# Hybrid decoder trunk on one core: token-major weight units of 4 k-tiles x 512 columns in place of 8 x 256, and new prices for TensorE in the scheduler

## Chip, core and metric

The kernel runs on one core of one Trainium2 chip. The metric is the device time of one execution in microseconds (us); lower is better. The kernel before takes 1906.26 us (median of three runs).

## The reference

Two layers over 256 tokens of width 1024, all in float32. Cut to its frame:

```python
for l in range(2):
    h = h + 0.5 * rmsnorm(swiglu(rmsnorm(h, g[0]), ffn1_gate[l], ffn1_up[l], ffn1_down[l]), g[1])   # width 2816
    u = rmsnorm(h, g[2])
    q, k, v, z, xBC, dt_raw, gate_pre = split(u @ w_in[l])       # 1536, 1536, 1536, 2048, 4096, 32, 2048 columns
    y_att = dilated_attention(q, k, v)                           # 3 dilation groups x 8 heads of 64
    y_ssd = ssd_branch(z, xBC, dt_raw, ...)                      # conv of 4 taps, silu, Mamba-2 SSD in 8 groups, gate by silu(z), norm
    gates = sigmoid(gate_pre + b_gate[l])
    h = h + rmsnorm((gates[0] * (y_att @ w_att_out[l]) + gates[1] * (y_ssd @ w_ssd_out[l])) @ w_o[l], g[3])
    h = h + rmsnorm(memory_cross_attention(rmsnorm(h, g[4]), rmsnorm(mem, mem_norm_g[l]), ...), g[5])   # 4 heads of 256
    h = h + 0.5 * rmsnorm(swiglu(rmsnorm(h, g[6]), ffn2_gate[l], ffn2_up[l], ffn2_down[l]), g[7])
```

## The kernel before

**Weights.** All weight matrices are cut into units of 1 MB ([128 partitions] x [2048 float32]). `PLAN` lists the units in the order in which they are used. A unit is brought in as two halves (`raw`, 512 KB each, three buffers), and each half is split into a high part `wh` (ScalarE, a copy to float32r) and a low part `wl` (VectorE, `raw - wh`). Five units fit at once (`NBUF`). Each product is three float32r matmuls (`mm3`): high x high, high x low, low x high.

**Two forms of product.** *Feature-major* (`feat_major`): the weight tile is the stationary operand, 256 tokens of `x` stream past it; q, k, bc, xs, most of the FFN's gate and up, xa_wq and xa_wk. *Token-major* (`tok_major`): a tile of `x` (128 tokens of one k-tile of 128 features) is stationary and the weight's columns stream past it; dt and v, the gates, z, xa_wv and the first two units (`FF_TOK`) of each FFN's gate and up. In the kernel before a token-major unit holds all 8 k-tiles of 256 columns, so a matmul streams 256 columns, and a unit is worked off for token block `t = 0` and then `t = 1`. The row units (`row_mm`: down, att_out, ssd_out, w_o, xa_wo) stream 512 columns of the weight past a tile of the hidden values, into tiles `acc`.

**Order.** One Python program writes the instructions of all engines. TensorE (PE) follows the main line; everything else (norms, evacuations, attention heads, SSD groups) runs in generator tasks that are advanced by `tick()`. Each engine has a clock of its own in the program, moved on by prices (`pe_cost`, `act_cost`, `dve_cost`, ...); a task's instruction is written down when its inputs are ready by these clocks (for PE: `MARGIN` = 300 ns earlier). So the prices decide behind which main-line matmul a task's transpose or matmul stands. On the chip each engine works its own list in order.

**Places that the prediction speaks of.** (a) *Norm chains*: after the last `acc` matmul of a row unit group, `boundary` computes, for each token block, squares (ACT), product with the gain (DVE, `pg`), root (POOL), new `h` (DVE), squares again, root, `xn` (DVE), and then PE transposes `xn` into `xT`. While the chain of `t = 1` runs, PE works on things that do not need it: the `t = 0` pass of the next FFN's first units (tile `gu`), of dtv and v, or, behind w_o, the values of the memory (tile `xv`, unit xa_wv). (b) *SSD groups* (`ssd`, `group_units`): for each of 8 groups the matmuls `BC` and `xs` are followed by a convolution and silu (tile `conv`, ACT and DVE), whose results PE takes up in `cb` and `xsT`; later `y` goes through a norm and is transposed (`yT`). (c) The *start*, where the first weights are still on their way.

```python
MARGIN = 300
def wait(*aps, tag="ps", n=1):
    while not has(tag, n) or PE.at(aps) + MARGIN > now():
        yield
```

Of the kernel before, what the change touches and what calls it, by code (L numbers as in the profile page):

```python
# [38 lines left out]
def ffn_plan(name, l):  # L39
    p = []  # L40
    for j in range(FF_UNITS):
        p += [(name + "_gate", l, j), (name + "_up", l, j)]
        if j == FF_TOK:
            p += [(name + "_down", l, i) for i in range(FF_TOK - 1)]
        if FF_TOK <= j <= FF_UNITS - SPLIT:
            p.append((name + "_down", l, j - 1))
    return p + [(name + "_down", l, FF_UNITS - SPLIT + i) for i in range(SPLIT)]


def plan():  # L50
    p = []
    for l in range(DEPTH):
        p += ffn_plan("ffn1", l)
        p += [("dtv", l, 0), ("dtv", l, 1)] + [("v", l, i) for i in (1, 3)]
        p += [("q", l, 2 * g) for g in range(3)] + [("k", l, 2 * g) for g in range(3)]
        p += [("v", l, i) for i in (0, 2, 4)]
# [13 lines left out]
        p += [("ssd_out", l, 7), ("xa_wk", l, 3), ("xa_wv", l, 0)] + [("w_o", l, u) for u in range(4)]  # L70
        p += [("xa_wv", l, 1), ("xa_wv", l, 2)] + [("xa_wq", l, u) for u in range(4)] + [("xa_wv", l, 3)]
# [3 lines left out]


PLAN = plan()


@with_exitstack  # L80
def tile_trunk(ctx: ExitStack, tc: tile.TileContext, x, mem, gains, hparams, chparams, b_gate, wts, out):
# [265 lines left out]
    def get(name, l, i):  # L347
# [8 lines left out]
        k, n = dict(dtv=(4, 1152)).get(name, (2 if name in ROWS else KB, 2048))  # L356
# [42 lines left out]
    def xk(xx, k, cols):  # L399
        tiles = xx[k // 2]  # L400
        return tiles[0][:, k % 2, cols], tiles[1][:, k % 2, cols]

# [127 lines left out]
    def ffn(name, l, xx, ready, make_chain, early=lambda: None):  # L530
# [10 lines left out]
        def act_tok(j, t, p):  # L541
            s = t2("hm0", (128, 256))
            yield from ACT("activation", s, p[:, 0], AF.Silu)
            yield from DVE("tensor_mul", s, s, p[:, 1])
            give(p)
            yield from wait(s)
            pt = ps("hT", (128, 2, 128))
            for i in range(2):
                yield from PE("transpose", pt[:, i], s[:, blk(i)], ident)
            yield from split(hts[j][0][:, :, tok(t)], hts[j][1][:, :, tok(t)], pt)  # L550
# [6 lines left out]
        w0 = [None] * FF_TOK  # L557
        for t in range(2):
            for j in range(FF_TOK):
                if t == 0:  # L560
                    w0[j] = [get(name + "_gate", l, j), None]
                    new_h(j)
                p = un("gu")
                tok_major(p[:, 0], w0[j][0], xx, t)
                if t == 0:
                    w0[j][1] = get(name + "_up", l, j)
                tok_major(p[:, 1], w0[j][1], xx, t)
                if t == 1:
                    drop(w0[j][0])
                    drop(w0[j][1])  # L570
                pend[j] = spawn(act_tok(j, t, p))
        acc = None

        def down(j):
            until(pend[j])
# [58 lines left out]
    def mix(l, xx, ready, params, kv):  # L634
# [66 lines left out]

        wd = {}
        for t in range(2):
# [8 lines left out]
            for j in (2, 4):  # L712
                if t == 0:
                    wd[j] = get("v", l, j - 1)
                p = un("v1", (128, 512))
                tok_major(p[:, :256], wd[j], xx, t)
                if t == 1:
                    drop(wd[j])
                spawn(evac_v(j, t, p, 0))
        decay_task = spawn(decays(dt_raw))  # L720

        def late_v():
            for i in (0, 2, 4):
                w = get("v", l, i)
                p = un("v")
                for t in range(2):
                    tok_major(p[:, t], w, xx, t)
                drop(w)
                spawn(evac_v(i + 1, None, p, 0))
# [105 lines left out]
        def gate_act(p, bg, u, res):  # L835
            g = t2("gate")
            yield from DVE("tensor_tensor", g, p, bg[:, None, u * 256:u * 256 + 256].to_broadcast([128, 2, 256]), op=ALU.add)
            give(p)
            yield from ACT("activation", g, g, AF.Tanh, scale=0.5)
            res[u] = g  # L840

        def gate_unit(which, bg, u, res):
            w = get(f"gate{which}", l, u)
            p = un("gate")
            for t in range(2):
                tok_major(p[:, t], w, xx, t)
            drop(w)
            spawn(gate_act(p, bg, u, res))

        m0, g1 = [None] * 4, [None] * 4  # L850
        bg = gate_bias(0)
        for u in range(4):
            gate_unit(0, bg, u, m0)
        bg = gate_bias(1)
        gate_unit(1, bg, 0, g1)
# [17 lines left out]
        def z_gate(p, res):  # L873
            zt = t2("zt")
            yield from ACT("activation", zt, p, AF.Silu)
# [3 lines left out]
        def decay_block(g, W, cbm, rz):  # L879
# [11 lines left out]
            while not rz:  # L891
# [8 lines left out]
        def ssd(g, rBC, rxs, rz, yy):  # L900
# [4 lines left out]
            decay = spawn(decay_block(g, W, cbs, rz))  # L905
# [50 lines left out]
            while not rz:  # L956
                yield
            yield from DVE("tensor_tensor", y[:, 1], y[:, 1], yo, op=ALU.add)
            yield from DVE("tensor_tensor", y, y, rz[0], op=ALU.mult)
# [23 lines left out]
        def group_units(g):  # L983
            rBC, rxs, rz, yy = [], [], [], []
# [11 lines left out]
            w = get("z", l, g)  # L996
            p = un("z")
            for t in range(2):
                tok_major(p[:, t], w, xx, t)
# [288 lines left out]
```

## Time and profile before

| | |
|---|---|
| runs | 1905.03, 1906.26, 1909.02 us (median 1906.26) |
| profiled execution, first to last instruction (its span) | 1903.0 us; its own whole time is not given beside it, the runs' median is 3.3 us above the span |
| TensorE matmul busy | 1880.4 us, 99% of the span, 13620 matmul records |
| TensorE weight load busy | 93% |
| VectorE / ScalarE / GpSimd busy | 63% / 52% / 11% |
| granted TensorE clock, mean | 0.999 of full |
| HBM traffic | 330.9 MB, mean 174 GB/s over the span |

Matmuls are pipelined and their recorded durations overlap (a 256-column matmul has a duration of 283 ns and the next one starts 120 ns later), so what a matmul costs is read from the distance between starts, not from its duration or the busy share.

### The profile page before, as it was taken

What the parts mean: (1) busy time and instruction counts of PE and PEld (TensorE: products, weight loads), DVE (VectorE), ACT (ScalarE), POOL (GpSimd) and SP (SyncE); (2) the same over time, 40 slices, a digit from 0 to 9 for tenths busy, and PEclk for the clock granted to TensorE, in tenths of its full rate; (3) what the DMA queues carried; (4) which work ended last, traced back from release to release, by engine and by line L of the source; (5) the groups of instructions that cost most, each with busy time, mean ns of one, the idle gap of its engine ahead of it and who ended that gap; (6) DMA issues with size and microseconds to landing.
All of it is one profiled execution on the core that took longest, in us unless ns stands there. A gap on an engine that the chain in (4) does not pass through costs nothing.

```text
span 1903.0 us, 33128 instructions
## 1 busy us (share of the span) xinstructions
PE 1880.4 (99%) x13620; PEld 1763.9 (93%) x13620; DVE 1192.1 (63%) x1729; ACT 995.9 (52%) x1488; POOL 212.2 (11%) x244
## 2 busy tenths in 40 slices
PE   7999999999999999999999999999999999999998
PEld 6999899899999989999999999898999999999997
DVE  5555654568787865655465546535878777765553
ACT  5444654456666654544354436444566664654542
POOL 0000000032342000000000000000332420000000
PEclk9999999999999999999999999999999999999999
DMA  6655453355565554565556546443555556545652
GB/s 212 217 192 194 158 186 116 118 174 181 182 198 170 172 199 145 175 218 184 178 177 218 182 160 210 134 156 121 166 190 176 168 189 207 171 139 176 223 192 77
DMA packets 107720, 333.09 MB, mean 175 GB/s; under 512 B 10864, under 2 KB 27568, under 8 KB 107568
## 3 DMA queue, kind: packets, MB, share of 16 engines
q1 hardware_dynamic: 107568, 330.97, 53.3%
q8 instruction: 107, 1.75, 0.4%
q14 instruction: 45, 0.37, 0.1%
HBM read 329.81 MB, written 1.11 MB: 174 GB/s over the span
## 4 chain that ended last, share of the span: by engine, by line
PE 92%; DVE 2%; DMA 2%; ACT 2%; POOL 1%; issue 1%; SPq 0%; DVEq 0%; POOLq 0%; ACTq 0%
PE acc L210 22%; PE u L210 11%; PE g L210 11%; PE gate L210 5%; PE xs L210 5%; PE gu L210 4%; PE z L210 4%; PE BC L210 4%; PE q L210 4%; PE k L210 4%; PE v L210 2%; PE xq L210 2%; PE o L210 2%; DMA raw<-in_wts 2%; PE xv L210 2%; PE xk L210 2%
## 5 line engine op out<-in xcount | busy, mean ns | idle before, releaser
L210 DVE TENSOR_TENSOR wl<-raw,wh 128x1024 fp32r<-128x1024 f32 (+1 forms) x588 | 704.9, 1216 | 332.1 <-ACT wh L210 330.1
L210 ACT ACTIVATE wh<-raw 128x1024 fp32r<-128x1024 f32 (+1 forms) x588 | 610.2, 1050 | 443.6 <-DMA raw<-in_wts 231.9
L210 POOL TENSOR_SCALAR ab<-ab,nacs 128x128 f32<-128x128 f32 x128 | 134.4, 1066 | 465.4 <-DMA ab<-acsD 465.4
L210 PE MATMUL g<-xTh,wh 128*128 128x256 f32 x576 | 163.2, 283 | 0.0
L210 PE MATMUL u<-xTh,wh 128*128 128x256 f32 x576 | 163.0, 283 | 0.0
L210 PE MATMUL u<-xTl,wh 128*128 128x256 f32 x576 | 163.0, 283 | 0.0
L210 PE MATMUL u<-xTh,wl 128*128 128x256 f32 x576 | 163.0, 283 | 0.0
L210 PE MATMUL g<-xTh,wl 128*128 128x256 f32 x576 | 163.0, 283 | 0.0
L210 PE MATMUL g<-xTl,wh 128*128 128x256 f32 x576 | 163.0, 283 | 0.0
L210 PE MATMUL acc<-wl,hth 128*128 128x512 f32 x352 | 137.5, 390 | 0.0
L210 PE MATMUL acc<-wh,htl 128*128 128x512 f32 x352 | 137.4, 390 | 0.0
L210 PE MATMUL acc<-wh,hth 128*128 128x512 f32 x352 | 137.3, 390 | 0.0
L210 PEld LDWEIGHTS g<-xTl,wh 128*128 128x128 f32 x576 | 110.5, 192 | 0.9
L210 PEld LDWEIGHTS g<-xTh,wh 128*128 128x128 f32 x576 | 110.5, 192 | 0.9
L210 PEld LDWEIGHTS u<-xTh,wh 128*128 128x128 f32 x576 | 110.6, 192 | 0.0
L210 PEld LDWEIGHTS u<-xTl,wh 128*128 128x128 f32 x576 | 110.6, 192 | 0.0
L210 PEld LDWEIGHTS u<-xTh,wl 128*128 128x128 f32 x576 | 110.6, 192 | 0.0
L210 PEld LDWEIGHTS g<-xTh,wl 128*128 128x128 f32 x576 | 110.5, 192 | 0.0
L210 DVE SCALAR_TENSOR_TENSOR conv<-raw_xbc,chp,conv 128x255 f32<-128x255 f32 (+2 forms) x192 | 81.9, 488 | 0.0
L210 PEld LDWEIGHTS acc<-wh,htl 128*128 128x128 f32 x352 | 66.1, 188 | 13.7
L210 PEld LDWEIGHTS acc<-wh,hth 128*128 128x128 f32 x352 | 66.2, 188 | 12.9
L210 PEld LDWEIGHTS acc<-wl,hth 128*128 128x128 f32 x352 | 66.2, 188 | 12.7
(260 smaller groups left out, 5169.5 us busy)
## 6 DMA issues: line engine op xcount, KB each, us to landing
raw<-in_wts SPq DMA_DIRECT2D x580, 512.0 KB, 4.5
gain<-in_gains SPq DMA_DIRECT2D x18, 512.0 KB, 6.4
ab<-acsD SPq DMA_DIRECT2D x32, 256.0 KB, 6.0
raw<-in_wts SPq DMA_DIRECT2D x8, 288.0 KB, 3.4
gain<-in_b_gate SPq DMA_DIRECT2D x4, 512.0 KB, 6.8
mem<-in_mem SPq DMA_DIRECT2D x8, 256.0 KB, 4.9
out_h<-h SPq DMA_DIRECT2D x4, 256.0 KB, 2.7
h<-in_x SPq DMA_DIRECT2D x2, 256.0 KB, 2.9
```

Source lines behind the costliest of these rows:

```text
L210: return getattr(self.eng, what)(*a, **k)
```

## The change

1. **Layout.** A token-major unit (`WIDE`: z, both gates, xa_wv, the values but for 512 of the 1536 columns, and the first two gate and up units of each FFN) holds 4 k-tiles of 512 columns. Two units make one block of 512 columns: a pass over token block `t` takes the first unit's four k-tiles and then the second's, into one PSUM tile of 128 x 512. Both units stay until `t = 1` is through. Bytes, number of units, splits and DMAs are as before.
2. **What follows from it.** z comes in blocks of two groups (after `xs` of the even groups), gate1 in two blocks (before the groups, and after group 3), the memory's values in two blocks of two heads (the first with the keys, the second behind w_o; before, two units stood behind w_o and one behind the queries). The silu of the FFN's first units and the merges work on 128 x 512. `y * silu(z)` becomes two multiplies of 256 in place of one of 512.
3. **Prices.** `pe_cost`: a float32r matmul of n columns is priced at n/2.4 + 13.4 ns, before n/2.4 + 2.5; transposes and float32 matmuls change by little.

```diff
@@ def plan()
-        p += [("gate0", l, u) for u in range(4)] + [("gate1", l, 0)]
+        p += [("gate0", l, u) for u in range(4)] + [("gate1", l, u) for u in range(2)]
...
-            p.append(("z", l, g))
-            if g in (2, 4, 6):
-                p.append(("gate1", l, g // 2))
+            if g % 2 == 0:
+                p += [("z", l, g), ("z", l, g + 1)]
+            if g == 3:
+                p += [("gate1", l, 2), ("gate1", l, 3)]
...
+WIDE = ("vw", "gate0", "gate1", "z", "xa_wv")
+
+def wide(name, i):
+    return name in WIDE or name.endswith(("_gate", "_up")) and i < FF_TOK
@@ def pe_cost(op, out, ins, k)
+        m, n = size(ins[0]), size(ins[1])
         if op == "transpose":
-            cycles = 256
-        elif ins[0].dtype == F32R:
-            cycles = size(ins[1])
-        else:
-            m = size(ins[0])
-            cycles = 4 * max(m, size(ins[1])) * (m / 128 if m == 64 else 1)
-        return cycles / 2.4 + 2.5
+            return 109
+        if ins[0].dtype == F32R:
+            return n / 2.4 + 13.4
+        return 2 * max(112, 2 * n / 2.4 + (28 if m == 64 else 3))
@@
+    def wide_units(name, l, b, xx, done):
+        ws = [get(name, l, 2 * b)]
+        for t in range(2):
+            p = un(name, (128, 512))
+            tok_major(p, ws[0], xx, t, 0, 4)
+            if t == 0:
+                ws.append(get(name, l, 2 * b + 1))
+            else:
+                drop(ws[0])
+            tok_major(p, ws[1], xx, t, 4, 4)
+            if t == 1:
+                drop(ws[1])
+            done(t, p)
@@ def ffn(...)
         for t in range(2):
-            for j in range(FF_TOK):
...
-                tok_major(p[:, 0], w0[j][0], xx, t)
...
-                tok_major(p[:, 1], w0[j][1], xx, t)
...
+            for m in ("_gate", "_up"):
+                p = un("gu", (128, 512))
+                for i in range(2):
+                    if t == 0:
+                        w0[m].append(get(name + m, l, i))
+                    tok_major(p, w0[m][i], xx, t, 4 * i, 4)
+                    if t == 1:
+                        drop(w0[m][i])
@@ def group_units(g)
-            w = get("z", l, g)
-            p = un("z")
-            for t in range(2):
-                tok_major(p[:, t], w, xx, t)
-            drop(w)
-            spawn(z_gate(p, rz))
+            if g % 2 == 0:
+                wide_units("z", l, g // 2, xx, lambda t, p: spawn(z_gate(p, rz)))
@@
         value(1)
-        value(2)
-        O, heads = xattn(l, xq, K, V, value)
+        O, heads = xattn(l, xq, K, V)
```

**Where the instructions stand, first place: TensorE behind w_o of layer 0**, where the values of the memory (`xv` before, `xa_wv` in the change) run while the chain of `t = 1` computes `xn`; `xT` are the transposes that take `xn` up. Before, 72 rows of `xv` stand between the last `acc` row of w_o and the first of these rows' `xT`:

```order
L210 MATMUL xv<-wh,memh 128x256
L210 MATMUL xv<-wl,memh 128x256
L210 MATMUL xv<-wh,meml 128x256
L210 MATMUL xT<-ident,xn 128x128 x4
L210 MATMUL xv<-wh,memh 128x256
L210 MATMUL xv<-wl,memh 128x256
```

In the change 33 rows of `xa_wv` stand there, of twice the columns:

```order
L215 MATMUL xa_wv<-wh,memh 128x512
L215 MATMUL xa_wv<-wl,memh 128x512
L215 MATMUL xa_wv<-wh,meml 128x512
L215 MATMUL xT<-ident,xn 128x128 x4
L215 MATMUL xa_wv<-wh,memh 128x512
L215 MATMUL xa_wv<-wl,memh 128x512
```

The first `xT` of `t = 1` moved from behind 72 x 256 columns to behind 33 x 512. In the same way it stands behind 33 `gu` rows in place of 72 at the first units of ffn2 (both layers) and of ffn1 in layer 1; behind dtv it stands after 24 rows `dtv` and 24 of `v` (512 columns) in place of 24 `dtv` and 42 of `v` (256). The chains of `t = 0`, which run behind the last 48 `acc` rows, are taken up after 26 `acc` rows in place of 28 at w_o (both layers).

**Second place: VectorE in the same stretch**, the chain of `t = 1` itself (`h_93` is the half of `h` that belongs to `t = 1`; `wl` rows are weight halves between its steps). Before:

```order
L210 TENSOR_TENSOR pg<-acc,gain 128x512
L210 TENSOR_TENSOR wl<-raw,wh 128x1024
L210 TENSOR_TENSOR pg<-acc,gain 128x512
L210 SCALAR_TENSOR_TENSOR h_93<-pg,r,h_93 128x512
L210 TENSOR_TENSOR wl<-raw,wh 128x1024
L210 SCALAR_TENSOR_TENSOR h_93<-pg,r,h_93 128x512
L210 TENSOR_TENSOR wl<-raw,wh 128x1024
L210 SCALAR_TENSOR_TENSOR xn<-h_93,r,gain 128x512 x2
```

In the change:

```order
L215 TENSOR_TENSOR pg<-acc,gain 128x512
L215 TENSOR_TENSOR wl<-raw,wh 128x1024
L215 TENSOR_TENSOR pg<-acc,gain 128x512
L215 SCALAR_TENSOR_TENSOR h_93<-pg,r,h_93 128x512
L215 TENSOR_TENSOR wl<-raw,wh 128x1024
L215 SCALAR_TENSOR_TENSOR h_93<-pg,r,h_93 128x512
L215 TENSOR_TENSOR wl<-raw,wh 128x1024
L215 SCALAR_TENSOR_TENSOR xn<-h_93,r,gain 128x512 x2
```

Nothing moved on VectorE: the same three weight halves stand between the same steps. The same holds at the first units of ffn2 in both layers, of ffn1 in layer 1, and behind w_o in layer 1.

**Third place: TensorE in SSD group 2 of layer 0**, between the end of ssd_out (`acc<-..,yh`) and `cb`, which takes up the convolution of `BC`. Before (nine more `xs` rows follow, and then `cb`):

```order
L210 MATMUL acc<-wh,yh 128x512
L210 MATMUL acc<-wl,yh 128x512
L210 MATMUL acc<-wh,yl 128x512
L210 MATMUL xs<-xTh,wh 128x256
L210 MATMUL xs<-xTl,wh 128x256
L210 MATMUL xs<-xTh,wl 128x256
L210 MATMUL yT<-ident,y 128x128 x4
L210 MATMUL xs<-xTh,wh 128x256
L210 MATMUL xs<-xTl,wh 128x256
L210 MATMUL xs<-xTh,wl 128x256
```

In the change:

```order
L215 MATMUL acc<-wh,yl 128x512
L215 MATMUL xs<-xTh,wh 128x256
L215 MATMUL xs<-xTl,wh 128x256
L215 MATMUL xs<-xTh,wl 128x256
L215 MATMUL xs<-xTh,wh 128x256
L215 MATMUL xs<-xTl,wh 128x256
L215 MATMUL xs<-xTh,wl 128x256
L215 MATMUL cb<-conv 128x128 x2
```

`cb` moved from behind 15 `xs` rows (and the transposes `yT`, which now stand among the `BC` rows ahead) to behind 6. In group 0, `xsT` stands after 22 rows of `z` (512 columns) and `cb` in place of 48 rows of `z` (256), `cb` and 3 of the next `BC`.

## Rows read from the trace of the kernel before

**Rows 1.** The page of the profile: TensorE's line of the busy times, and the chain that ended last as shares of the span by engine.

```profile
PE 1880.4 (99%) x13620; PEld 1763.9 (93%) x13620; DVE 1192.1 (63%) x1729; ACT 995.9 (52%) x1488; POOL 212.2 (11%) x244
PE 92%; DVE 2%; DMA 2%; ACT 2%; POOL 1%; issue 1%; SPq 0%; DVEq 0%; POOLq 0%; ACTq 0%
```

**Rows 2.** The timeline of TensorE in the middle of ffn2, layer 0: start in us from the span's start, duration, engine, line, operation, output and inputs, shape. 24 matmuls of 512 columns start from the first row to just before the second, 48 of 256 columns from the third to just before the fourth.

```profile
827.48 0.40 PE L210 MATMUL acc<-wh,hth 128*128 128x512 f32 x1
...
832.95 0.28 PE L210 MATMUL g<-xTh,wh 128*128 128x256 f32 x1
...
838.70 0.28 PE L210 MATMUL u<-xTh,wh 128*128 128x256 f32 x1
...
844.46 0.40 PE L210 MATMUL acc<-wh,hth 128*128 128x512 f32 x1
```

**Rows 3.** Groups of TensorE's instructions by name and shape: the high x high third of each token-major group (xcount; busy us, mean ns of one; idle before).

```profile
L210 PE MATMUL gate<-wh,xTh 128*128 128x256 f32 x256 | 76.1, 297 | 0.0
L210 PE MATMUL gu<-wh,xTh 128*128 128x256 f32 x256 | 74.9, 293 | 1.7 <-ACT wh L210 1.7
...
L210 PE MATMUL z<-wh,xTh 128*128 128x256 f32 x256 | 73.1, 285 | 0.0
...
L210 PE MATMUL v<-wh,xTh 128*128 128x256 f32 x160 | 47.3, 296 | 2.5 <-ACT v L210 2.5
...
L210 PE MATMUL xv<-wh,memh 128*128 128x256 f32 x128 | 36.7, 287 | 0.0
```

**Rows 4.** The timelines of TensorE and VectorE at the start: the last two waits of the `t = 0` pass for a weight half (in brackets the idle time before, and what ended it), and the split of that pass's last half.

```profile
27.28 0.39 PE L210 MATMUL gu<-wl,xTh 128*128 128x256 f32 x1 [0.87 <-DVE wl L210]
...
29.43 0.39 PE L210 MATMUL gu<-wl,xTh 128*128 128x256 f32 x1 [0.46 <-DVE wl L210]
28.15 1.22 DVE L210 TENSOR_TENSOR wl<-raw,wh 128x1024 fp32r<-128x1024 f32 x1 [0.60 <-ACT wh L210]
```

**Rows 5.** Timelines at the start of dtv in layer 0: TensorE's first `dtv` row of `t = 0`, its wait at the second `v` unit, the first transposes of `t = 1`, the first `dtv` row of `t = 1`; and VectorE's `xn`.

```profile
207.60 0.29 PE L210 MATMUL dtv<-wh,xTh 128*128 128x288 f32 x1
...
215.37 0.39 PE L210 MATMUL v<-wh,xTh 128*128 128x256 f32 x1 [1.54 <-ACT v L210]
...
217.62 0.60 PE L210 MATMUL xT<-ident,xn 128*128 128x128 f32 x4
...
218.78 0.32 PE L210 MATMUL dtv<-wh,xTh 128*128 128x288 f32 x1
216.37 0.75 DVE L210 SCALAR_TENSOR_TENSOR xn<-h,r,gain 128x512 f32<-128x512 f32 x1 [0.85 <-POOL r L210]
```

**Rows 6.** Timelines at the five other norm chains of `t = 1`: TensorE's first row behind the last `acc`, VectorE's `xn` (two halves in one row), and for the first of them TensorE's transposes. In order: behind w_o in layer 0, ffn2 in layer 0, ffn1 in layer 1, behind w_o in layer 1, ffn2 in layer 1.

```profile
690.50 0.28 PE L210 MATMUL xv<-wh,memh 128*128 128x256 f32 x1
698.70 1.42 DVE L210 SCALAR_TENSOR_TENSOR xn<-h,r,gain 128x512 f32<-128x512 f32 x2 [1.04 <-POOL r L210]
699.51 0.66 PE L210 MATMUL xT<-ident,xn 128*128 128x128 f32 x4 [0.21 <-DVE xn L210]
768.67 0.28 PE L210 MATMUL gu<-wh,xTh 128*128 128x256 f32 x1
776.52 1.41 DVE L210 SCALAR_TENSOR_TENSOR xn<-h,r,gain 128x512 f32<-128x512 f32 x2 [0.84 <-POOL r L210]
958.18 0.28 PE L210 MATMUL gu<-wh,xTh 128*128 128x256 f32 x1
965.68 1.41 DVE L210 SCALAR_TENSOR_TENSOR xn<-h,r,gain 128x512 f32<-128x512 f32 x2 [0.84 <-POOL r L210]
1630.74 0.28 PE L210 MATMUL xv<-wh,memh 128*128 128x256 f32 x1
1638.24 1.41 DVE L210 SCALAR_TENSOR_TENSOR xn<-h,r,gain 128x512 f32<-128x512 f32 x2 [0.84 <-POOL r L210]
1708.22 0.28 PE L210 MATMUL gu<-wh,xTh 128*128 128x256 f32 x1
1715.54 1.42 DVE L210 SCALAR_TENSOR_TENSOR xn<-h,r,gain 128x512 f32<-128x512 f32 x2 [0.84 <-POOL r L210]
```

**Rows 7.** ScalarE inside the first of these chains: two weight halves that stand ahead of the squares of the new `h` on this engine and wait for their DMA.

```profile
692.99 1.06 ACT L210 ACTIVATE wh<-raw 128x1024 fp32r<-128x1024 f32 x1 [1.15 <-DMA raw<-in_wts]
695.34 1.06 ACT L210 ACTIVATE wh<-raw 128x1024 fp32r<-128x1024 f32 x1 [1.29 <-DMA raw<-in_wts]
```

**Rows 8.** The chain of `t = 0` at w_o, layer 0: VectorE's `xn` and TensorE's first transpose.

```profile
684.03 1.42 DVE L210 SCALAR_TENSOR_TENSOR xn<-h,r,gain 128x512 f32<-128x512 f32 x2 [1.91 <-POOL r L210]
685.00 0.38 PE L210 MATMUL xT<-ident,xn 128*128 128x128 f32 x2
```

**Rows 9.** SSD in layer 0, TensorE and ScalarE. Group 2: TensorE's first row behind `BC`, the silu that ends its convolution, `cb`. Group 0: the first row behind `xs`, the silu of its convolution, `xsT`.

```profile
450.67 0.40 PE L210 MATMUL acc<-wh,yh 128*128 128x512 f32 x1
456.78 0.63 ACT L210 ACTIVATE conv<-conv 128x512 f32<-128x512 f32 x1
458.37 0.39 PE L210 MATMUL cb<-conv 128*128 128x128 f32 x2
403.10 0.28 PE L210 MATMUL z<-wh,xTh 128*128 128x256 f32 x1
408.40 0.63 ACT L210 ACTIVATE conv<-conv 128x512 f32<-128x512 f32 x1 [0.86 <-DVE conv L210]
409.77 0.38 PE L210 MATMUL xsT<-ident,conv 128*128 128x128 f32 x2
```

More of the change, by code (lines that the diff above doesn't have):

```diff
@@ L539, in act, with gate_tok, act_tok @@
             yield from split(*hts[j], s)
[L541 to L544, printed above, removed]
+        def gate_tok(res, p):
+            s = t2("hm0", (128, 512))
+            yield from ACT("activation", s, p, AF.Silu)
+            give(p)
+            res.append(s)
+        def act_tok(res, t, p):
+            while not res:
+                yield
+            s = res[0]
+            yield from DVE("tensor_mul", s, s, p)
             give(p)
             yield from wait(s)
[L547 to L550, printed above, removed]
+            pt = ps("hT", (128, 2, 2, 128))
+            for i in range(4):
+                yield from PE("transpose", pt[:, i // 2, i % 2], s[:, blk(i)], ident)
+            for j in range(2):
+                yield from split(hts[j][0][:, :, tok(t)], hts[j][1][:, :, tok(t)], pt[:, j])
             give(pt)
@@ L700, in evac_dt, with evac_vw @@
             yield from evac_v(0, t, p, 32)
+        def evac_vw(a, t, p):
+            for h_ in range(2):
+                if vt[a + 2 * h_] is None:
+                    vt[a + 2 * h_] = t2("v")
+                yield from ACT("activation", vt[a + 2 * h_][:, t], p[:, blk2(h_)], AF.Copy)
+            give(p)
         wd = {}
@@ L955, in ssd @@
             give(po)
-            while not rz:
+            while len(rz) < 2:
                 yield
             yield from DVE("tensor_tensor", y[:, 1], y[:, 1], yo, op=ALU.add)
-            yield from DVE("tensor_tensor", y, y, rz[0], op=ALU.mult)
+            for c in range(2):
+                yield from DVE("tensor_tensor", y[:, c], y[:, c], rz[c][:, g % 2], op=ALU.mult)
             ms = small("gms", [128, 2], 2)
@@ L1015, in merge0 @@
         def merge0(acc):
-            for u in range(4):
+            for b in range(2):
                 for t in range(2):
-                    yield from DVE("scalar_tensor_tensor", m0[u][:, t], m0[u][:, t], 1.0, acc[t][u // 2][:, blk2(u % 2)],
-                                                   op0=ALU.add, op1=ALU.mult)
-                if u % 2:
-                    give(acc[0][u // 2])
-                    give(acc[1][u // 2])
+                    yield from DVE("scalar_tensor_tensor", m0[t][b], m0[t][b], 1.0, acc[t][b], op0=ALU.add, op1=ALU.mult)
+                    give(acc[t][b])
         def attend():
@@ L1182, in key, with evac_v, value @@
             spawn(evac_kv(K, p))
-        def value(hd):
-            w = get("xa_wv", l, hd)
-            p = un("xv")
-            for t in range(2):
-                tok_major(p[:, t], w, mx, t)
-            drop(w)
-            spawn(evac_kv(V, p))
+        def evac_v(b, t, p):
+            hl = (t2("kvh", (128, 512), F32R), t2("kvl", (128, 512), F32R))
+            yield from split(*hl, p)
+            give(p)
+            V[b][t] = hl
+        def value(b):
+            V[b] = [None, None]
+            wide_units("xa_wv", l, b, mx, lambda t, p: spawn(evac_v(b, t, p)))
         kv = dict(norm=start_norm, key=key, value=value)
```

153 lines of the change are left out of this document (76 added, 77 removed).

## The prediction

> **What bounds the kernel.** I read the page first. The matmuls' line says 99% busy, and PE carries 92% of the chain that ended last [rows 1]. But recorded matmuls overlap, so a busy share of 99% cannot tell whether PE issues as fast as it can. The distance between starts can. In the middle of an FFN, with nothing waited for, 24 matmuls of 512 columns take 832.95 - 827.48 = 5.47 us, or 227.9 ns each, and 48 of 256 columns take 844.46 - 838.70 = 5.76 us, or 120.0 ns each [rows 2]. The columns alone, at 2.4 GHz (the granted clock is 0.999 of full over the span), would be 213.3 and 106.7 ns, so a matmul costs some 13 to 15 ns beside its columns, whatever its width. I then looked along PE's timeline for waits. Those I found are few: a few us at the start for weights [rows 4], 1.54 us behind dtv [rows 5], 0.2 us behind w_o [rows 6]. So the kernel is bound by PE's issue, with little idle time to win, and the reader should keep two things apart: what PE's work itself costs, and which of the other engines' results come only just in time. The second is invisible in the busy shares, and it is what the change disturbs.
>
> **Term 1: fewer, wider matmuls.** The groups that change are gate, gu, z, xv and four of the five v units per layer: 256 + 256 + 256 + 128 + 4/5 of 160 = 1024 matmuls of the high x high kind [rows 3]. There are three kinds, so 3072 matmuls of 256 columns become 1536 of 512. A pair costs 240.0 ns now, a wide one 227.9 ns by the nearest row, which has the same shape and the same role of the operands (128 tokens stationary, a weight row of 512 streaming) [rows 2]. The saving is 12.1 ns x 1536 = **18.6 us**. Weight loads per matmul stay the same and have more time to hide. Bytes, splits and DMAs are unchanged.
>
> The Trainium skill bears on this term (TensorE: Matmul & The Clock Gate, section Back-to-back issue gap): it gives a gap of N/2.4 + 2.5 ns, so merging two matmuls would save only 2.5 ns, an estimate of 3.8 us in all. The rows disagree with that constant for float32r here, with 13 to 15 ns [rows 2], and the measurement decides.
>
> **Term 2: the norm chains of t = 1.** While such a chain runs, PE has a fixed stretch of other work, and this stretch shrinks, but the chain doesn't: on VectorE the same weight halves stand between the same steps. At w_o in layer 0 the chain's `xn` starts at 698.70 and the transposes, which waited for it, start at 699.51, so a first half of `xn` is usable 0.81 us after its row starts. From PE's first row behind `acc` that is 699.51 - 690.50 = 9.01 us [rows 6]. PE's 72 rows ahead of the transposes took 72 x 0.120 = 8.64 us, so it waited about 0.37 us. In the change 33 rows of 512 columns stand there: 33 x 0.2279 = 7.52 us, and PE waits 1.49 us. The other four chains by the same reckoning [rows 6]: ffn2 in layer 0 776.52 + 0.81 - 768.67 = 8.66; ffn1 in layer 1 8.31; w_o in layer 1 8.31; ffn2 in layer 1 8.13. All four were in time or nearly so before 8.64 us, and now wait 1.14, 0.79, 0.79 and 0.61 us. Sum 4.82 us, less the 0.37 of before: **4.5 us lost**. Can the chain get shorter? Part of it is ScalarE standing at weight halves that wait 1.15 and 1.29 us for their DMA [rows 7]; the transfers don't come earlier, so I assume no. Its bounds are 0 (every chain 1.5 us shorter) and 7 us (0.5 us longer each).
>
> Behind dtv, in both layers, the same chain is the limit already: usable at 216.37 + 0.81 = 217.18, 9.58 us after dtv's first row. The new stretch is 3.2 us for dtv (24 matmuls of 288 columns at 288/2.4 + 13.3 ns, between the two prices of [rows 2]) + 24 x 0.2279 = 8.67 us, so PE waits 0.9 us there; but the 1.54 us wait for the evacuation of dtv's tile goes, as the tile is now asked for only after 5.5 us of `v`, where before it was 2.9 us [rows 5]. The start of dtv for `t = 1`, 11.18 us after the first row now, comes out some 0.4 us earlier, which is about the share of term 1 that lies there. Nothing is added or lost.
>
> **Term 3: the chains of t = 0.** At w_o they are usable at 684.03 + 0.81 = 684.84, and PE came at 685.00 [rows 8]. Two `acc` rows fewer are 0.456 us, so it waits 0.30 us, in both layers; the three others by the same shift at most as much. I take **0.9 us lost**, between 0 and 1.5.
>
> **Term 4: SSD.** PE takes up each group's results at `cb`, `xsT` and `yT`, 48 places in all. The new prices make the program's PE clock some 10% slower (120.1 in place of 109.2 ns for 256 columns) while ACT and DVE keep theirs, so a PE consumer is written fewer matmuls behind its producer. Two places in numbers [rows 9]. `cb` of group 2: PE's stretch behind `BC` was 458.37 - 450.67 = 7.70 us, the convolution was done 456.78 + 0.63 - 450.67 = 6.74 us into it. In the change the stretch is 24 x 0.2279 + 6 x 0.120 = 6.19 us: a wait of 0.55 us. `xsT` of group 0: stretch 6.67 us, convolution done at 5.93 us; now 22 x 0.2279 + 0.55 for `cb` (what 51 x 0.120 leaves of the old 6.67) = 5.56 us: a wait of 0.37 us. Other groups have more work in between (group 5's memory norm, the z blocks of two groups), and since three chains are always in flight, a wait at one gives the others slack. ScalarE and VectorE lists change here too, so the chains themselves may get shorter. Bounds: 0, and 48 x 0.46 = 22 us if every place were like these two. I take one wait of 0.25 us per group, nearer the lower end for those reasons: **4.0 us lost**.
>
> **Term 5: the start.** The `t = 0` pass of the first four units follows the arrival of the weights; its last half is split only at 28.15 + 1.22 = 29.37 us, and PE waits for it at 29.43 [rows 4]. So of these four units' saving (4 x 0.29 us) the `t = 0` half is lost: **0.6 us lost**. The rest of the evacuations is hidden: the same bytes through ACT and DVE, which are 52% and 63% busy. Uncovered, the 16 multiplies in `y` that become two of half the width would add a few tenths of a us in all.
>
> **Sum.** -18.6 + 4.5 + 0.9 + 4.0 + 0.6 = -8.6 us: the span of 1903.0 becomes 1894.4, and with the 3.3 us that lie between the span and the runs' median, **1897.7 us**. What one can tell from no change in this kernel is about 0.2%, or 3.8 us.
>
> **Rivals.**
> - *The saving arrives nearly whole.* The chains turn out 0.5 to 1 us shorter, because fewer weight halves per us of program time compete for ACT and DVE. For: the chain at ffn2 in layer 1 is already 0.9 us shorter than that at w_o in layer 0, with the same order on DVE [rows 6]. Against: DVE's order is unchanged. Time: terms 2 to 4 at a fifth, 1906.3 - 18.6 + 1.9 + 0.6 = 1890.
> - *The second unit of a block comes late.* A block needs its second unit 2.7 us after the first, where before it was 5.8 us. For: ACT waits over 1 us for weight halves at w_o [rows 7], which come 2.35 us apart there (695.34 - 692.99), 4.7 us for a unit. Against: a block of two units takes PE 10.9 us, so two fit, and behind the start no wait of PE for a weight stands among those I found. Each of the 24 blocks late by 0.3 us would take 7 us: 1905, no change.
> - *Slower, by SSD.* The waits of term 4 are as long as in the two places worked out, at nearly all 48, and add up to 17 to 22 us. From (18.6 - 6.0)/48 = 0.26 us a place on, nothing is left. For: both samples lie above that. Against: the overlap of the chains. At 0.4 us: 1906.3 - 12.6 + 19 = 1913.
> - *Width buys nothing in these units.* A matmul of 512 columns costs two of 256, 240 ns, against the one row that I have (227.9). Then terms 2 to 4 remain, smaller by the longer stretches: about +6 us, 1912. The skill's constant of 2.5 ns would come near to this case, at 3.8 us saved and, by the same losses, about 1912 too.
>
> **Chances.** The forecast (1893 to 1902) 0.50; the whole saving 0.20; late units, or the losses just eating the gain (1902.5 to 1910) 0.17; slower by SSD 0.09; no gain from width 0.04. Faster by over 0.2% therefore about 0.72, within it 0.16, slower 0.12. The range that leaves out no more than 2 in 10 goes from the whole saving to the losses at the upper part of their bounds: 1888 to 1905, and for the forecast alone 1893 to 1902.
>
> **What the changed profile would show.** Term 1: about 12080 matmul records, `gate`, `gu`, `z`, `xa_wv` at 512 columns starting 227 to 229 ns apart. Term 2: idle time of 0.6 to 1.5 us ahead of the first `xT` of `t = 1` behind w_o, ffn2 and ffn1, with `xn` as its releaser; the 1.54 us wait at `v` gone and one of about 0.9 us at `xT` in its place. Term 4: waits of 0.2 to 0.6 us at `cb`, `xsT` or `yT` in some groups. Term 5: the first `g` row about 0.6 us earlier than now. Wrong would make it above all a price of the wide matmul other than 228 ns (each ns is 1.5 us), chains that change length, or idle time ahead of the second unit of a block, with `wh` or `wl` as its releaser.

## The result, and the profile after

The changed kernel takes 1927.65 us (median of 4, 1925.93 to 1930.73) against 1907.64 us for the kernel before (4 runs): a ratio of 1.0100, 95% interval 1.0077 to 1.0124. It is 1% slower, outside the predicted range on the far side. The profiled execution has a span of 1929.0 us where that of before had 1903.0, so 26.0 us have to be found. First the page of the changed kernel, TensorE's busy line and the chain that ended last:

```profile
PE 1877.1 (97%) x12084; PEld 1678.9 (87%) x12084; DVE 1187.6 (62%) x1713; ACT 993.8 (52%) x1484; POOL 202.5 (10%) x244
PE 77%; DMA 8%; DVE 7%; ACT 5%; issue 2%; POOL 2%; SPq 0%; DVEq 0%; POOLq 0%; ACTq 0%
```

1536 matmul records fewer [rows 1], as announced. But PE's share of the chain fell from 92% to 77%, and DMA, DVE and ACT now have 20% of it. This points away from the matmuls, but it is weak evidence by itself: in gates_gu_v below, which is faster than the kernel before, PE's share is 82%. The price of a matmul is read from TensorE's timeline behind w_o; from the first row to the second are 20 intervals:

```profile
712.36 0.39 PE L215 MATMUL xa_wv<-wh,memh 128*128 128x512 f32 x1
...
716.89 0.39 PE L215 MATMUL xa_wv<-wh,meml 128*128 128x512 f32 x1
```

(716.89 - 712.36)/20 = 226.5 ns; the prediction took 227.9. Then the waits of TensorE, summed by who waits for whom (us in total, times, longest), of the changed kernel:

```profile
PE xT L215 <- DVE xn L215: 23.6, 12, 9.4
PE xsT L215 <- ACT conv L215: 7.8, 7, 2.1
PE pa L215 <- DVE a L215: 3.0, 2, 1.5
PE gu L215 <- DVE wl L215: 2.9, 5, 1.3
PE gu L215 <- ACT wh L215: 1.4, 1, 1.4
PE cb L215 <- ACT conv L215: 1.0, 1, 1.0
PE xs L215 <- DVE xql L215: 1.0, 2, 0.5
PE yT L215 <- ACT y L215: 1.0, 2, 0.7
PE dtv L215 <- ACT xTh L215: 0.9, 2, 0.5
PE mT L215 <- DVE m L215: 0.9, 2, 0.6
PE hT L215 <- DVE hm L215: 0.8, 2, 0.5
PE y L215 <- DVE ab L215: 0.5, 1, 0.5
```

The same view of the kernel before:

```profile
PE xT L210 <- DVE xn L210: 8.8, 2, 8.6
PE v L210 <- ACT v L210: 2.5, 2, 1.5
PE gu L210 <- DVE wl L210: 2.5, 4, 0.9
PE gu L210 <- ACT wh L210: 1.7, 2, 1.4
PE xsT L210 <- ACT conv L210: 0.4, 2, 0.2
```

39 waits with 44.8 us in place of 12 with 15.9 us: 28.9 us more. (The longest in each, 9.4 and 8.6 us, is the start of the program.) Where the biggest of them stand is in TensorE's timeline; in order the chain of `t = 0` at w_o in both layers, the chains of `t = 1` at w_o and ffn2 in layer 0, the one behind dtv in layer 0, and `pa`, the running sum of SSD's decays:

```profile
703.79 1.12 PE L215 MATMUL xT<-ident,xn 128*128 128x128 f32 x4 [3.30 <-DVE xn L215]
1653.85 0.66 PE L215 MATMUL xT<-ident,xn 128*128 128x128 f32 x4 [3.29 <-DVE xn L215]
720.34 0.66 PE L215 MATMUL xT<-ident,xn 128*128 128x128 f32 x4 [0.35 <-DVE xn L215]
794.08 0.63 PE L215 MATMUL xT<-ident,xn 128*128 128x128 f32 x4 [1.60 <-DVE xn L215]
...
218.23 0.63 PE L215 MATMUL xT<-ident,xn 128*128 128x128 f32 x4 [1.86 <-DVE xn L215]
...
237.22 0.63 PE L215 MATMUL pa<-a,causal 128*128 128x32 f32 x4 [1.46 <-DVE a L215]
```

A second loss stands in no wait. This is TensorE's timeline around the first of them, and the windows over it (length, busy time and count of PE, PEld, DVE, ACT, POOL, then the granted clock PEclk, DMA share, GB/s):

```profile
700.11 0.39 PE L215 MATMUL acc<-wl,mh 128*128 128x512 f32 x1
...
705.13 0.63 PE L215 MATMUL acc<-wh,mh 128*128 128x512 f32 x1
705.56 0.63 PE L215 MATMUL acc<-wl,mh 128*128 128x512 f32 x1
703.00:705.00 2.00, 1.21 (x5) 1.21 (x6) 2.00 (x3) 1.79 (x3) 0.00 (x0) 0.50 0.00 0
705.00:707.00 2.00, 2.00 (x6) 1.52 (x6) 2.00 (x4) 0.71 (x2) 0.00 (x0) 0.50 0.13 47
707.00:709.00 2.00, 2.00 (x9) 1.60 (x8) 0.34 (x1) 0.21 (x1) 0.00 (x0) 0.50 0.95 303
709.00:711.00 2.00, 2.00 (x10) 1.62 (x9) 1.80 (x3) 0.56 (x2) 0.00 (x0) 0.91 0.48 174
```

While TensorE waits for `xn` the granted clock falls to 0.50, the lower of its two levels (1.2 GHz), and it is back only at about 709.4. Until then the `acc` rows start 0.43 us apart, not 0.23. From the end of the wait on that is about (0.5 x 1.2) + (0.5 x 2) + (0.5 x 2) + (0.09 x 2) = 2.8 us on top of the 3.3 us of the wait itself. The same is seen at 237 to 242, 1194 to 1198 and 1654 to 1660, 1.7 us each by the same reckoning: some 8 us in all. In the kernel before there is no such stretch between the start and the last microseconds.

So: -18.6 us of matmul (-20.7 at 226.5 ns), +28.9 us of waits, +8 us of clock make +18 (+16) of the +26 us. A bracket is about 0.15 us shorter than the gap that it stands for (703.79 - 700.11 - 0.23 = 3.45 against 3.30), which for 27 more waits is another 4 us. The remaining 4 us or more lie in gaps that these views don't list.

### The profile page after: what moved, and what is told of

The parts are those of the page before. It is cut to its first block, busy times and chain, and to the rows that moved or that the text cites. A ratio compares the mean times of both kernels' runs of the same rounds, so it can differ in the third digit from the quotient of the medians.

```text
span 1929.0 us, 30083 instructions
## 1 busy us (share of the span) xinstructions
PE 1877.1 (97%) x12084; PEld 1678.9 (87%) x12084; DVE 1187.6 (62%) x1713; ACT 993.8 (52%) x1484; POOL 202.5 (10%) x244
## 4 chain that ended last, share of the span: by engine, by line
PE 77%; DMA 8%; DVE 7%; ACT 5%; issue 2%; POOL 2%; SPq 0%; DVEq 0%; POOLq 0%; ACTq 0%
PE acc L215 18%; PE u L215 11%; PE g L215 11%; DMA raw<-in_wts 7%; PE gate L215 5%; PE k L215 4%; DVE wl L215 3%; PE xs L215 3%; PE q L215 3%; PE z L215 3%; PE BC L215 3%; ACT wh L215 2%; PE o L215 2%; PE gu L215 2%; PE sc L215 2%
```

## The experiments

The change has two parts, a layout and a price list for TensorE, so the runs set them apart, then look into each. All ratios are to the kernel before in runs on the same chip.

| run | layout | prices | median us | ratio (95%) |
|---|---|---|---|---|
| prices_only | before | new | 1921.55 | 1.0091 (1.0074-1.0109) |
| prices_margin_900 | before | new, MARGIN 900 | 1927.35 | 1.0106 (1.0088-1.0124) |
| prices_all_10 | before | new, ACT and DVE +10% | 1910.53 | 1.0020 (1.0009-1.0031) |
| prices_dma_1900 | before | new, transfers +1 us | 1912.70 | 1.0034 (1.0021-1.0047) |
| wide_old_prices | all but z | old | 1908.64 | 1.0011 (1.0001-1.0022) |
| gates_gu_v | gates, gu, v | old | 1901.27 | 0.9965 (0.9953-0.9977) |
| gates_gu | gates, gu | old | 1903.13 | 0.9978 (0.9968-0.9989) |
| xv_narrow | all but xa_wv | new | 1925.83 | 1.0113 (1.0099-1.0128) |
| z_narrow | all but z | new | 1927.93 | 1.0113 (1.0095-1.0131) |
| margin_600 | all | new, MARGIN 600 | 1923.64 | 1.0095 (1.0081-1.0109) |
| gates_gu_v_new | gates, gu, v | new | 1926.32 | 1.0101 (1.0087-1.0115) |
| gates_gu_v_all_10 | gates, gu, v | new, ACT and DVE +10% | 1906.42 | 0.9999 (0.9990-1.0007) |
| gates_gu_v_new_dma_1900 | gates, gu, v | new, transfers +1 us | 1904.34 | 0.9991 (0.9981-1.0001) |
| wide_at_492 | gates, gu, v | old, 512 at 492 cycles | 1899.22 | 0.9965 (0.9953-0.9978) |
| wide_492_dma_1900 | gates, gu, v | the same, transfers +1 us | 1917.37 | 1.0061 (1.0045-1.0076) |

**The prices without the layout.** In the kernel before only `pe_cost` is replaced, by that of the change.

> The kernel before with nothing but the new prices of TensorE in its scheduler; every unit stays narrow. Theory P (the new prices take the time: they make the planner's TensorE clock run about 10% slower in the 256-column stretches, so transposes are put that many rows earlier and the results of ScalarE and VectorE come late): the waits of the changed kernel appear here without the saving, about 1907.6 + 35 = 1940 us, with waits of 1 to 2 us each at xT<-xn and at xsT<-conv. Theory L (the layout takes it: buffers held longer and larger units): within 5 us of 1907.6, and those waits as short as before.

1921.55 us, 15 us slower, with not one instruction changed in kind or number. Theory P's sign holds. Its 35 us were too many, and the waits at `xT` (behind the start) and `xsT` are 0.3 to 0.9 us each, where it named 1 to 2. Two lines of the waits show which kind of step suffers:

```profile
PE xT L208 <- DVE xn L208: 11.7, 8, 8.4
...
PE pa L208 <- DVE a L208: 1.7, 2, 1.0
```

The whole list has 24 waits with 22.9 us, against 12 with 15.9 us before. These 7.0 us are half of the 14.1 us by which the profiled spans differ (1917.1 and 1903.0 us). By the distances between starts some 4 us more stand ahead of and among the transposes `xT` and `yT`, in gaps too short for the list; where the rest stands was not found.

**The layout without the prices.** The changed kernel with the old `pe_cost`, z in its narrow units for the reason that the expectation gives; so there is no run of the whole layout at the old prices.

> The changed kernel with the old prices of TensorE, and with z left in narrow units, since with wide z and the old prices the buffers of the plan block one another and no program comes out. 1152 of the 1536 pairs are wide: 1152 x 12.1 ns = 13.9 us saved. Theory P: 1907.6 - 13.9 + about 5 for the norm chains = 1899 us, or 1905 if the 3.4 us waits at the t=0 chains of w_o belong to the buffers. Theory L: the waits of the changed kernel stay, some 1925 to 1930 us.

1908.64 us: 3.6 us above the 1905 that theory P names for the case that the waits at w_o stay, and 19.3 us below the same layout with the new prices (z_narrow). Of its waits two of 2.85 us at the `t = 0` chain of w_o, one in each layer, stand out: they stayed.

**xa_wv narrow.** In the changed kernel (two places of the edit; the code that reads the values follows them):

```diff
-        p += [("ssd_out", l, 7), ("xa_wk", l, 3), ("xa_wv", l, 0), ("xa_wv", l, 1)] + [("w_o", l, u) for u in range(4)]
+        p += [("ssd_out", l, 7), ("xa_wk", l, 3), ("xa_wv", l, 0)] + [("w_o", l, u) for u in range(4)]
...
-WIDE = ("vw", "gate0", "gate1", "z", "xa_wv")
+WIDE = ("vw", "gate0", "gate1", "z")
```

> The changed kernel with xa_wv alone put back to narrow units of 256 columns, in the places of before; all else, the prices too, as changed. Its value block ahead of w_o then holds 2 tiles of the 28 and not 4. Theory B (the squares of the t=0 chain of w_o wait for a tile that is still read by the w_o matmuls): the wait of the first transposes at w_o t=0 falls from 3.45 us to 0.3 us in both layers, 6.3 us less, against 192 pairs x 12.1 ns = 2.3 us of width given up: 1927.7 - 4 = 1923.6 us. Without B (the chain is late for another reason): those waits stay above 2.5 us and the time is 1930 us.

The two waits fall from 3.45 us to 0.3 us (696.46 - 695.93 - 0.23 in layer 0), as theory B has it. The rows that matter are TensorE's first row of w_o, a later one, and ScalarE's first square of the chain, in the changed kernel:

```profile
683.56 0.39 PE L215 MATMUL acc<-wh,mh 128*128 128x512 f32 x1
...
696.71 0.39 PE L215 MATMUL acc<-wl,mh 128*128 128x512 f32 x1
697.19 0.60 ACT L215 ACTIVATE junk<-acc 128x512 f32<-128x512 f32 x1 [8.66 <-PE acc L215]
```

With xa_wv narrow, the first row of w_o, the square, and TensorE's last row ahead of the transposes and the transposes:

```profile
679.36 0.40 PE L215 MATMUL acc<-wh,mh 128*128 128x512 f32 x1
689.11 0.60 ACT L215 ACTIVATE junk<-acc 128x512 f32<-128x512 f32 x1 [6.94 <-PE acc L215]
...
695.93 0.39 PE L215 MATMUL acc<-wl,mh 128*128 128x512 f32 x1
696.46 0.66 PE L215 MATMUL xT<-ident,xn 128*128 128x128 f32 x4
```

With xa_wv narrow w_o's first row starts at 679.36 and the square 9.75 us later: 42 rows of 0.227 us are 9.5 us, and its accumulator is complete after 42 rows. In the changed kernel w_o starts at 683.56 and the square comes 13.63 us later. That is right behind the end of row 59 (696.71 + 0.39 = 697.10), the row of `t = 1` that reads the `mh` tile of w_o's first unit for the last time. `squares` takes a tile from the pool of 28 (`NT2`). K holds 8, the memory's halves 8, `mm` 8 and a wide value block 4, so none is free until w_o's first unit gives its own back; a narrow value unit leaves two. The planner counts no tiles of this pool, so it puts the transposes where the squares would have ended. In time little of this came through: waits at `xsT` rose from 7.8 to 9.7 us, and the ratio is the changed kernel's within the intervals. So this wait is explained, but the run doesn't show that the 20 us hang on it.

**A larger MARGIN.** `MARGIN = 600` in the changed kernel.

> The changed kernel with MARGIN, the time by which the planner wants an operand finished before it puts a transpose or a small matmul into TensorE's row, at 600 and not 300. Theory P: the transposes stand about 300 ns later in the row, so of the 30 us that they wait in the changed kernel at xT<-xn, xsT<-conv, yT and mT a good part goes: about 1907 to 1915 us, with the waits at xsT<-conv under 0.5 us. Theory L: 1925 to 1935 us, the waits as in the changed kernel.

1923.64 us, not told apart from the changed kernel by its ratio; theory P's 1907 to 1915 us did not come. The waits at `xsT` fall from 7.8 to 4.8 us, but others come (`yT` 2.1, `xs` 2.9 us).

**Fewer wide units, old prices.** With gates, first FFN units and values wide, and then without the values:

> Old prices; the gates, the first FFN units and the values wide, z and xa_wv narrow: 960 pairs, 960 x 12.1 ns = 11.6 us of matmul less than before. Beside the run with xa_wv wide as well (1908.6 us) the theory of the buffers takes away its two waits of 3.0 us at the t=0 chain of w_o and gives back 2.3 us of width: 1908.6 - 6.0 + 2.3 = 1904.9 us, with those waits under 0.5 us. If the waits are put there by something else they stay, and the time is 1909 to 1911 us.

> Old prices; only the gates and the first FFN units wide: 768 pairs, 9.3 us of matmul less than before. The two waits of 1.3 and 1.4 us at xT<-xn of the dtv block and the two of 0.6 us behind them, which came with the wide values, go, and before's waits at v (1.7 and 1.1 us) come back: 1904.9 - 3.9 + 2.8 + 2.3 = 1906.1 us if the widths cost little else where they stand; 1900 us if a larger part of the waits belonged to the values; above 1908 us if the wide gates themselves (the 2.1 us wait of cb behind them) cost more than they save.

Both are faster than the kernel before, by 0.35% and 0.22%. The first came 3.6 us below the expectation, the second 3.0 us; with xa_wv narrow the waits at w_o are absent here too. The values gain a little or nothing, as their intervals overlap.

**z narrow, new prices.**

> The changed kernel with z alone put back to one narrow unit in each group; the new prices and all other widths stay. Theory Z (two wide z units in every second group bring their weights and their results in pairs, and conv on ScalarE stands behind them): the waits at xsT<-conv fall from 8.9 us to about the 3.3 us of the prices-only run, 5.6 us less against 384 pairs x 12.1 ns = 4.6 us given up, so 1926.7 us. Theory P alone (the prices put the xsT transposes early in any layout): the waits stay near 9 us and the time is 1932 us.

The waits at `xsT` fall from 7.8 to 4.3 us, in the direction of theory Z, and the time stays the same, as the 4.6 us of width that the expectation counts go with them. So wide z is about neutral, and the theories are not told apart by the time.

**What in the prices costs.** Two attempts to give the cover back on the narrow layout, with the new `pe_cost` as it is. The first raises the prices of ScalarE and VectorE by a tenth, the second is a larger fixed margin (`MARGIN = 900`). The first edit:

```diff
-        return t + n + 93 * ("accum_out" in k) + 93 * scalars(ins)
+        return 1.1 * (t + n + 93 * ("accum_out" in k) + 93 * scalars(ins))
...
-        return 70 + per * size(ins[0]) + 60 * scalars(ins)
+        return 1.1 * (70 + per * size(ins[0]) + 60 * scalars(ins))
```

> The kernel before with the new prices of TensorE and with the prices of ScalarE and VectorE raised by a tenth too, so that all three engines stand to one another much as in the kernel before. Theory P says that only this relation sets the row: about 1907 us (1904 to 1911), the waits at xT<-xn and yT back under 2 us in all. If the new prices cost time in another way (the order among TensorE's own kinds, or weights fetched at another moment), it stays near the 1921.6 us of the prices-only run.

> The prices-only kernel with MARGIN 900 in the place of 300. If the cover that the new prices took away can be given back as a fixed time ahead of each transpose, this comes back to about 1908 us, with the waits at xT<-xn and yT under 2 us. If the cover has to grow with the length of the chain, and has to reach the rows of ScalarE and VectorE too, which MARGIN does not touch, it gives back only a part: 1913 to 1918 us.

The first gives 11 of the 15 us back, so the relation of the engines' prices matters and not TensorE's alone. The second gives nothing back (1927.35 us; its interval overlaps that of prices_only), where the expectation had 1918 us at most. This speaks against a fault that lies only in where transposes stand in TensorE's row. ScalarE's row shows another place. In prices_only, around the exponential `sp_e` that the decays need:

```profile
230.19 1.06 ACT L208 ACTIVATE wh<-raw 128x1024 fp32r<-128x1024 f32 x1 [1.65 <-DMA raw<-in_wts]
...
232.56 0.26 ACT L208 ACTIVATE sp_e<-sp_e 128x64 f32<-128x64 f32 x1
```

A weight half that is not there yet stands ahead of the exponential; ScalarE waits 1.65 us for it, and `pa` is 1.03 us late. The planner lets a transfer land 1100 + 1456 + 900 = 3456 ns after it can be issued; the trace has 4.5 us (median of 580). If TensorE's short price used to cover this error, the transfer priced by the trace should do so too:

```diff
-    DMA = Engine("DMA", nc.sync, dma_cost, 900, 1e9, 0)
+    DMA = Engine("DMA", nc.sync, dma_cost, 1900, 1e9, 0)
```

> The prices-only kernel with one more price set by the trace: a transfer of a weight half is planned to land 1100 + 1456 + 1900 = 4456 ns after it could be issued, and not 3456; the trace has 4.5 us from issue to landing. Theory D (with exact prices for TensorE the planner puts weight halves into ScalarE's row before they have landed, and what stands behind them on that engine, such as the exponential ahead of pa, comes late): most of the 15.5 us come back, 1908 to 1912 us, and the wait at pa goes. Theory S alone (only a planner whose TensorE is too fast leaves cover, wherever the error lies): a change of the transfers' price gives back little, 1918 us or more.

1912.70 us, 9 of the 15 us back, 0.7 us above theory D's range. In ScalarE's row the half that stood ahead of the exponential stands behind it (231.16), the exponential starts 1.69 us earlier, and `pa` waits for nothing. In the kernel before, the two rows stand in this order too, at 230.88 and 231.17. With the longer transfers:

```profile
230.87 0.26 ACT L208 ACTIVATE sp_e<-sp_e 128x64 f32<-128x64 f32 x1
...
231.16 1.04 ACT L208 ACTIVATE wh<-raw 128x1024 fp32r<-128x1024 f32 x1
```

But this is not the whole of it. In prices_all_10, which got more back, a late half still stands ahead of the exponential, and `pa` waits 1.15 us:

```profile
229.03 1.06 ACT L208 ACTIVATE wh<-raw 128x1024 fp32r<-128x1024 f32 x1 [2.12 <-DMA raw<-in_wts]
```

So what comes back does not hang on this one place. Common to both runs is that no wait is left at `xT` behind the start (11.7 - 8.4 = 3.3 us in prices_only).

**The same on the wide layout.** gates_gu_v with the new prices, with the new prices and ACT and DVE a tenth higher, and with the new prices and the longer transfers:

> The layout of gates_gu_v with the new prices of TensorE. On the narrow kernel they cost 15 us. If layout and prices add: 1901.3 + 15 = 1916 us. If the layout makes the prices dearer, because a wide unit leaves fewer places where a transpose can be put later: 1920 us or more; if the exact price of the wide matmuls is the smaller step (5% and not 9%): 1911 to 1914 us.

> The layout of gates_gu_v with the new prices of TensorE, and ScalarE and VectorE priced a tenth higher. Theory S: as the run with 492 cycles, up to what the unscaled waits of the planner (semaphores, DMA, GpSimd) leave short: 3.5 us above it as on the narrow kernel, 1900 to 1902 us. If the new prices lose time otherwise than by the relation of the engines: 1910 us or more.

> The gates_gu_v layout with the new prices of TensorE, and the transfers priced 1 us longer as in the run before. Theory D: of the 25 us that the new prices cost on this layout most come back, 1903 to 1910 us. Theory S alone: 1920 us or more.

Here the new prices cost 25 us. One constant of the transfers gives 22 of them back, inside theory D's range and far from theory S's. ScalarE and VectorE a tenth higher give 20 back, to 1906.42 us, which lies between what its two theories named. So the transfers' price is shown as one cause of the loss, and not as the only one. TensorE's waits with the new prices, without and with the longer transfers:

```profile
PE xT L214 <- DVE xn L214: 15.8, 10, 8.2
...
PE pa L214 <- DVE a L214: 3.2, 2, 2.1
```

```profile
PE xT L214 <- DVE xn L214: 12.7, 6, 9.4
```

Behind the start (the longest in each) the waits at `xT` fall from 7.6 to 3.3 us, and those at `pa` are gone.

**The other way round.** In gates_gu_v at the old prices a 512-column matmul is priced 5% short of the trace and one of 256 columns 9%. One line evens that out, and a last run adds the longer transfers to it.

```diff
-            cycles = size(ins[1])
+            cycles = min(size(ins[1]), 492)
```

> The gates_gu_v kernel with one number changed: a matmul of 512 columns is priced at 492 cycles, 207.5 ns, and not at 215.8 ns. The old prices put a 256-column matmul at 109.2 ns where the trace has 120.0 (9% short) and one of 512 at 215.8 where it has 227.9 (5% short); now both are 9% short. Theory S (what covers late results is the share by which the planner's TensorE is too fast): the waits that gates_gu_v still has (xsT 2.6, xT 2.0, mT 1.6, pa 1.0, hT 1.9 us) fall by about half: 1901.3 - 4 = 1897 us. If those waits belong to the wide units and not to the prices: 1900 to 1903 us.

> The kernel with 512 columns at 492 cycles and the transfers priced 1 us longer. Its TensorE is 9% too fast in the plan, so a transfer of 3.46 us in the plan is 3.8 us on the chip, against 4.5 us measured: theory D says that some late results remain for this reason and go now, 1 to 3 us less, 1896 to 1898 us. Theory S alone: the same as without it, 1899 us, or slower by some us because weights are now taken late.

The first has the lowest median, 1899.22 us, but its ratio is that of gates_gu_v: not told apart, though its profile shows fewer waits (`xsT` 0.4 us against 1.9). The second missed its expectation by 19 us. Three lines of its waits:

```profile
PE acc L216 <- DVE wl L216: 3.7, 7, 0.8
PE xk L216 <- DVE wl L216: 2.6, 2, 1.3
...
PE acc L216 <- ACT wh L216: 2.2, 2, 1.3
```

Now TensorE waits for the weights themselves: taken for late by two errors that add up, the halves seem to stand too far back on ScalarE and VectorE (read from these releasers, not from a run of its own). Too early they block the chains, too late the matmuls. So theory D as I put it was too simple: the transfers' price has to fit TensorE's, and the old pair, both too short, fitted.

**Best.** gates_gu_v and wide_at_492 beat both kernels, at 0.9965 of the kernel before.

## Why the prediction was wrong

**The step that failed** is the account of the losses. Terms 2 to 5 moved PE's consumers forward and left the chains, and the rows of ScalarE and VectorE, nearly as they were; that made 10.0 us. The runs show two things in its place. The new prices alone cost 15 us, with the layout untouched. And at w_o the chain of `t = 0`, which term 3 left as it was, began 17 rows later in layer 0, by inference for want of a tile.

**Term 1** was nearly right: 226.5 ns where 227.9 was taken, and 12084 records. The rival of no gain from width is out. So is, for these matmuls, the constant of 2.5 ns that the prediction quotes from the Trainium skill (TensorE: Matmul & The Clock Gate, section Back-to-back issue gap).

**Term 2** was nearly right. At the five places the chain is ready 7.99, 9.15, 7.98, 7.99 and 8.03 us after TensorE's first row behind `acc`, where I took 9.01, 8.66, 8.31, 8.31 and 8.13, and the waits are 0.35, 1.60, 0.43, 0.34 and 0.48 us: 3.2 us less the 0.2 of before [rows 6], where I had 4.5. Behind dtv I took no loss; 2.5 us went at `v`, and 2.65 at `xT` and 0.9 at the first `dtv` rows came.

**Term 3** was missed by most: 0.9 us with a bound of 1.5. It measured 6.6 us of waits and 4.5 of clock. I shortened the stretch of [rows 8] by two rows and left the chain as it was. The wide value block takes two tiles more, which can be read from the code and the pool's 28, and that moved the chain's first step from behind row 42 to behind row 59 of w_o.

**Term 4** comes next: 4.0 us taken, and `xsT`, `cb`, `yT` and `y` make 10.3 us less 0.4. I gave its two worked samples (0.55 and 0.37 us [rows 9]) half their weight, but these two places don't wait at all. At `cb` of group 2 PE's stretch is 465.98 - 459.80 = 6.18 us, as forecast, and the convolution is done 5.29 us into it, not 6.74:

```profile
464.46 0.63 ACT L215 ACTIVATE conv<-conv 128x512 f32<-128x512 f32 x1
465.98 0.61 PE L215 MATMUL cb<-conv 128*128 128x128 f32 x4
```

At `xsT` of group 0 PE comes after 6.87 us and the convolution is done after 6.58. So the samples were no measure of the other places, where waits of up to 2.1 us stand. And the step under the term was too narrow. I read the new prices as moving PE's consumers some matmuls forward. They also move weight halves in ScalarE's row, against transfers whose price had not been touched. For this I had [rows 7], two halves standing ahead of a chain and waiting for their DMA, and used it only to say that the chain would not get shorter.

**Term 5** held: the first `g` row starts at 41.82 us in place of 42.79, 0.97 us earlier where 0.6 was taken, although the first transposes come 0.86 us later.

**What had no term.** `pa` (3.0 us), the memory's norm (23.6 less 9.4 and the rows above leaves about 1.7), `xs`, `mT` and `hT` (2.7): consumers of chains that had been in time by less than the cover. And the clock, some 8 us: I counted each wait at its face value.

**The rivals.** Slower by SSD had the right sign and was given 0.09; its price of 0.26 us a place would have been reached only with everything outside SSD added. Late second units are refuted: no such wait stands in the list behind the start. (There are 1536/48 = 32 blocks and not 24, so the price of that rival should have been 10 us.) The real rival was missing, that the prices alone, with no layout, cost 15 us.

**What stays open.** How the loss divides between prices and layout for wide z, and whether tiles for the value block would let xa_wv pay; neither was run. That the square waits for a tile is inferred from the row that it follows, the count of tiles and the narrow run. Part of the 15 us of prices_only stands in no listed wait. With the transfers' price set by the trace too, the new prices are still 6 us (narrow) and 3 us (wide) behind the old ones, for a reason that no run shows. And no run reorders the plan by a neutral edit, so how much of a difference of a few us between two plans is due to chance in their orders is unknown.

## What to carry to other kernels

A planner's prices are one set: correcting TensorE's alone took away the cover under an error of another (15 and 25 us here). So first compare every price with the trace, the transfers' time to landing among them, and change them together. Then measure: better prices are not yet a better plan, since gates_gu_v took 1904.34 us with both prices corrected and 1901.27 with both short. Cost a change of prices as an edit of its own, on the unchanged layout. And when a unit gets wider, count the buffers that its results hold at its busiest moment, in the pools that the planner doesn't watch.

## What was not expected of the hardware

A late operand can cost more than its wait. The granted clock fell to 0.50 at `pa` after a wait of 1.46 us, and at w_o after one of 3.30 us, and stayed there for several microseconds of full work, as in this window behind `pa` (columns as in the windows above):

```profile
239.00:242.00 3.00, 3.00 (x16) 3.00 (x17) 1.98 (x4) 2.41 (x3) 0.00 (x0) 0.54 0.56 193
```

It did not always fall: in wide_old_prices TensorE waited 2.85 us at the same place in w_o, and rows start 0.23 us apart right behind:

```profile
694.18 0.66 PE L216 MATMUL xT<-ident,xn 128*128 128x128 f32 x4 [2.85 <-DVE xn L216]
...
695.38 0.39 PE L216 MATMUL acc<-wl,mh 128*128 128x512 f32 x1
695.60 0.39 PE L216 MATMUL acc<-wh,ml 128*128 128x512 f32 x1
```

The Trainium skill (TensorE: Matmul & The Clock Gate, section What's actually happening) says that the lower clock is the default and that activity lifts it; the rows agree in so far as each fall in the changed kernel comes during a wait or shortly behind one, and each rise follows work.
